# NSA attention on one Trainium2 core: two compressed softmaxes of the second query half moved later, and output banks begun by their first product

## Chip, cores and metric

The kernel runs on one core of one Trainium2 chip. The metric is the device time of one execution in microseconds (us); lower is better.

## What is computed

A trunk of four layers (256 tokens, width 1024, fp32) with a mixer, an MLP and a gate per layer. Only the second layer's mixer, NSA attention, is touched by the change. Cut to what matters:

```python
def nsa_attention(h, w_in, cmp_pe, cmp_w1, cmp_w2, w_out, rel_bias):
    proj = h @ w_in                       # q: 16 heads of 64; k, v for three branches, 4 groups; gates
    kc = compress(k_cmp, ...); vc = compress(v_cmp, ...)      # 15 compressed blocks
    s_c = einsum(qc, kc) * scale + b_c
    p_c = masked_softmax(s_c, m_c)
    o_c = einsum(p_c, vc)
    ...                                   # selected blocks: 4 blocks, all taken
    p_s = masked_softmax(s_s, m_s); o_s = einsum(p_s, v_g)
    p_w = masked_softmax(s_w, m_w); o_w = einsum(p_w, vw)     # window of 512, holds all 256 tokens
    return gate0 * o_c + gate1 * o_s + gate2 * o_w            # then @ w_out
```

## The kernel before, in words

The four query heads of two groups form a query half `ap` (0 or 1), the 256 tokens two tiles `t` of 128 queries. An **item** (`ap`, `t`, `j`) is one pair of heads in one tile: its first part takes the scores of the selected and the window branch for both heads (L1002, two matmuls into two `acc` banks) and their softmaxes (`soft`: on DVE an addition of the bias that also gives the row maximum, L497, two per bank; on ACT the exponential, L501). Its second part comes three items later: DVE makes the gated reciprocals (L1008, L1010) and multiplies (L1019), PE transposes (L1022, into `wk` banks), ACT copies (L1024), PE multiplies by the values (L1031) into the output bank `po4[ap, t]` (a `pj` bank), which takes all four items of a half and tile. Items of tile 0 have 128 keys (score rows of 256 columns for the two branches), those of tile 1 have 256 (512 columns). In order of issue: 0 (0,0,0), 1 (0,0,1), 2 (0,1,0), 3 (0,0,2), 4 (0,1,1), 5 (0,0,3), 6 (0,1,2), 7 (0,1,3), 8 (1,1,0), 9 (1,1,1), 10 (1,0,0), 11 (1,1,2) and so on.

The **compressed softmax** of a half and tile (`cmp_soft`, called s`ap``t` below) has PE take eight small score products (L956), DVE add the bias (L959, twice), take the minimum (L963), subtract (L964), ACT exponentiate (L965), DVE sum (L967), invert (L968), gate (L969) and multiply (L973, twice); a second step, t`ap``t`, transposes on PE (L979) and copies on ACT (L980). `finish` adds the compressed branch's product (L1038) to the output bank and splits the bank into two parts (L755 on ACT, L756 on DVE).

Work that belongs to no item is issued between items by a table, `FILL`: after item number n it issues the pieces named there: s and t as above, q1 (half of the query projection of the second half: 48 matmuls, L173 to L175 into a `pj` bank, and ACT's copy L944), p (a part of the projection of the next gate, 6 matmuls L173 to L175 into an `acc` bank, copied by ACT at L1142), c, g, d (the compression), O (loads of the output weights, split by ACT L150 and DVE L151). Each engine runs its instructions in one order; a scheduler that knows priorities and estimated durations sets it from the order of issue, so a change of the table also moves other instructions. Banks (`acc` 4, `pj` 2, `wk` 2) are taken in turn: a matmul into a bank waits for the last reader of what was there before.

Before the change the first matmul of an output bank (L1013) is a product of zeros over all 512 columns, with `start=True`; all later ones add.

Of the kernel before, what the change touches and what calls it, by code (L numbers as in the profile page):

```python
# [23 lines left out]
HD = 64  # L24
# [9 lines left out]
PACC = {0: 1, 1: 1, 2: 1, 3: 1}  # L34
PCB = 2
CW = 2
FILL = {-2: 'q0.c.p.q0.c', 1: 'p.g', 2: 'd0.q1.s01.d1', 3: 's00', 4: 't00.q1', 5: 's10.p.s11', 6: 'p', 7: 't01', 11: 't11.t10.O', 16: 'p'}
NORM = {0: 1, 1: 2, 2: 3, 3: 3}
MEP = 1
BANKS = dict(acc=('acc', 4), pj=('pj', 2), wk=('wk', 2))  # L40
# [40 lines left out]
def backwards(v):  # L81

    *rest, (step, n) = [list(z) for z in v.ap]
    return bass.AP(tensor=v.tensor, offset=v.offset + step * (n - 1), ap=[*rest, [-step, n]])


class Trunk:
# [533 lines left out]
    def scores(self, q, k, qs, w):  # L621
# [5 lines left out]
                self.nc.tensor.matmul(sc[c][:, hh * w : (hh + 1) * w], q[cs, hh, qs], k[cs, hh, :w], start=True, stop=True)  # L627
        return sc

    def pipeline(self, items):  # L630

        live = []
        for it in items:
            live.append(it)
            live = [g for g in live if next(g, self) is not self]
        while live:
            live = [g for g in live if next(g, self) is not self]
# [203 lines left out]
    def nsa(self, i, hT):  # L841
        nc, a = self.nc, self.a
# [15 lines left out]
        vs = [va[:, 0], va[:, 1]]  # L858
# [27 lines left out]
        def fill(n):  # L886
            for z in FILL.get(n, "").replace(".", " ").split():
                if z[0] == "c":
                    if "ph" not in cmp:
                        cmp["ph"] = self.cpsum()  # L890
                        cmp["up"] = self.compress_up(blks, cmp["ph"])
                    next(cmp["up"])
                elif z[0] == "g":
                    cmp["hid"] = self.compress_gelu(cmp["ph"])
                elif z[0] == "d":
                    self.compress_down(int(z[1]), cmp["hid"], (kcT, vcd)[int(z[1])])
                elif z[0] == "s":
                    soft2[z[1:]] = cmp_soft(int(z[1]), int(z[2]), qt[int(z[1])])
                    next(soft2[z[1:]])
                elif z[0] == "t":  # L900
                    next(soft2[z[1:]])
                    soft2[z[1:]] = None
                elif z[0] == "q":
                    next(qs[int(z[1])])
                elif z[0] == "p":
                    next(self.ple)
                elif z[0] == "Q":
                    q_load(int(z[1]))
                elif z[0] == "O":
                    self.early.append(self.unit(self.w_out, len(self.early), 1, 0, D))  # L910
            if n > 0:
                for ap, t in last:
                    if (ap, t) in po4 and soft2.get(f"{ap}{t}", 1) is None and n >= last[ap, t] + DP[i]:
                        finish(ap, t)

        qt, po4, soft2 = {}, {}, {}
        last = {(z[0], z[1]): n + 1 for n, z in enumerate(ORDN)}
        cmp = {}
        blks = [self.compress_blocks(kind, kvT[:, 2 * kind : 2 * kind + 2, :]) for kind in range(2)]
# [70 lines left out]
        def item(ap, t, j, qt, nbs):  # L990


            nk = t + 1
            w = nk * P
            qs = slice(t * P, (t + 1) * P)
            sc = self.acc()
            es = self.es([P, 2, 2, w])
            m, s = self.small([P, 4]), self.small([P, 4])
            rows = (j, j ^ 1)
            for g2, r in enumerate(rows):  # L1000
                hs = slice(g2 * HD, (g2 + 1) * HD)
                nc.tensor.matmul(sc[g2][:, : 2 * w].rearrange("p (z k) -> p z k", z=2), qt[hs, r, qs], ksw[hs, ap, :, :w], start=True, stop=True)  # L1002
            for g2, r in enumerate(rows):
                zs = slice(2 * g2, 2 * g2 + 2)
                self.soft(es[:, g2], lambda b: sc[g2][:, b * w : (b + 1) * w], 2, lambda b: backwards(nbs[g2][:, r, :w]), m[:, zs], s[:, zs])
            for _ in range(DP[i]): yield
            rs = self.small([P, 2, 2])
            nc.vector.reciprocal(rs.rearrange("p a b -> p (a b)"), s)  # L1008
            h0, h1 = 8 * ap + rows[0], 8 * ap + 4 + rows[1]
            nc.vector.tensor_tensor(rs, rs, gate[:, t, h0 : h1 + 1 : h1 - h0, 1:3], op=ALU.mult)  # L1010
            if (ap, t) not in po4:
                po4[ap, t] = self.pj()
                nc.tensor.matmul(po4[ap, t], self.zero[0:1, :], self.zero[0:1, 0:1].to_broadcast([1, 512]), start=True, stop=False)  # L1013
            ats = []
            for g2 in range(2):
                e = es[:, g2]
                pt = self.wk()
                for z in range(2):
                    nc.vector.tensor_scalar(e[:, z, :], e[:, z, :], rs[:, g2, z : z + 1], None, op0=ALU.mult)  # L1019
                    for kb in range(nk):  # L1020
                        zz = (z * nk + kb) * P
                        nc.tensor.transpose(pt[:, zz : zz + P], e[:, z, kb * P : (kb + 1) * P], self.ident)  # L1022
                at = self.m2([P, 2, nk, P])
                nc.scalar.activation(at.rearrange("p a b c -> p (a b c)"), pt[:, : 2 * w], AF.Copy)  # L1024
                ats.append(at)
            for z in range(2):
                for kb in range(nk):
                    for g2, r in enumerate(rows):
                        g = 2 * ap + g2
                        ov = po4[ap, t][(r % 2) * HD : (r % 2 + 1) * HD, (2 * g2 + r // 2) * P : (2 * g2 + r // 2 + 1) * P]  # L1030
                        nc.tensor.matmul(ov, vs[kb][:, z, g * HD : (g + 1) * HD], ats[g2][:, z, kb, :], start=False, stop=False)  # L1031

        def finish(ap, t):
            rows = slice(ap * HD, (ap + 1) * HD)
            for g2 in range(2):
                for r in range(4):
                    ov = po4[ap, t][(r % 2) * HD : (r % 2 + 1) * HD, (2 * g2 + r // 2) * P : (2 * g2 + r // 2 + 1) * P]
                    nc.tensor.matmul(ov, vcd[rows, 2 * ap + g2, :], pcT[rows, t, r, :], start=False, stop=g2 == 1 and r > 1)  # L1038
            self.split_out(po4.pop((ap, t)).rearrange("p (a b) -> p a b", a=4), oT, 4 * ap, 4, t)
# [7 lines left out]
        def items():  # L1047
            n = 0
            nbs = {}
            fill(-1)  # L1050
            for ap, t, j in ORDN:
                if ap not in nbs:
                    nbs[ap] = [self.bias_load(8 * ap + 4 * g2) for g2 in range(2)]
                yield item(ap, t, j, qt[ap], nbs[ap])
                n += 1
                fill(n)
            yield fin()
# [198 lines left out]
```

## Time and profile before

| | us |
|---|---|
| three runs, median (lowest to highest) | 1389.82 (1389.5 to 1394.78) |
| the profiled execution, its own time | 1391.37 |
| its span in the trace | 1389.5 |
| PE busy in it | 1370.0 |
| DVE busy | 906.8 |
| ACT busy | 757.3 |
| the NSA attention stage in the trace | about 397 to 490 |

A span is the time from the first to the last instruction of the trace. Busy is the time in which an engine had an instruction under way. The trace counts two records for one fp32 matmul whose product is taken with 64 rows or 64 columns of the array (an item's score products, its value products), so that a pair of score products shows as x4.

### The profile page before, as it was taken

The page shows a single profiled execution, that of the slowest core. Times are in us where ns is not written, and L with a number is a line of the kernel's source. Part 1 is how long each engine was busy: PE and PEld are TensorE (multiplying, and loading weights), DVE is VectorE, ACT ScalarE, POOL GpSimd, SP SyncE. Part 2 cuts the span into 40 slices and gives each one's busy share as a digit, 9 for nine tenths or more (in the row PEclk, how much of TensorE's full clock was granted, in tenths as well). Part 3 has the DMA queues.
Part 4 walks back from the last instruction along what each step waited for, and adds up shares of the span by engine and source line. Part 5 has one row for each costly group of instructions (what it writes and reads, how often), then busy time and mean ns, then how long its engine had stood idle before and what let it go on. Part 6 is the DMA issues. An engine that isn't in the chain of part 4 may idle for free.

```text
span 1389.5 us, 20335 instructions
## 1 busy us (share of the span) xinstructions
PE 1370.0 (99%) x7604; PEld 1137.7 (82%) x7604; DVE 906.8 (65%) x1636; ACT 757.3 (55%) x1268; POOL 53.3 (4%) x101
## 2 busy tenths in 40 slices
PE   8999999999999999999999999999999999999998
PEld 6987888888976688888878878888888987888887
DVE  6677765667557666666575566766576677766655
ACT  6555555455446845454465665545556566554443
POOL 1011000002000000000010000000001011000000
PEclk9999999999999999999999999999999999999999
DMA  8844765546673046565466625656554753665642
GB/s 280 264 139 156 235 200 184 182 155 188 186 263 111 21 139 222 168 210 176 129 212 202 220 75 184 215 184 198 191 182 128 232 165 103 219 210 172 203 140 76
DMA packets 144526, 247.28 MB, mean 178 GB/s; under 512 B 10195, under 2 KB 101243, under 8 KB 144428
## 3 DMA queue, kind: packets, MB, share of 16 engines
q1 hardware_dynamic: 134848, 235.26, 52.5%
q10 hardware_dynamic: 9580, 10.73, 2.5%
q8 instruction: 60, 0.98, 0.3%
q14 instruction: 38, 0.31, 0.1%
HBM read 243.81 MB, written 1.10 MB: 176 GB/s over the span
## 4 chain that ended last, share of the span: by engine, by line
PE 88%; issue 5%; DVE 2%; ACT 2%; POOL 2%; DMA 1%; DVEq 0%; POOLq 0%; ACTq 0%
PE pj L182 13%; PE acc L173 13%; PE acc L174 13%; PE acc L175 13%; PE pj L183 7%; PE pj L173 6%; PE pj L175 6%; PE pj L174 6%; PE wk L256 2%; PE pj L1031 1%; PE acc L627 1%; DVE wl L151 1%; PE wk L1022 1%; PE acc L1002 1%; PE wk L744 1%
## 5 line engine op out<-in xcount | busy, mean ns | idle before, releaser
L151 DVE TENSOR_TENSOR wl<-raw,wh 128x1024 fp32r<-128x1024 f32 x421 | 510.5, 1221 | 227.7 <-ACT wh L150 215.1
L150 ACT ACTIVATE wh<-raw 128x1024 fp32r<-128x1024 f32 x421 | 443.7, 1059 | 224.3 <-PE acc L174 106.3
L182 PE MATMUL pj<-big,wh 128*128 128x512 f32 x768 | 274.1, 401 | 0.0
L183 PE MATMUL pj<-big,wl 128*128 128x256 f32 x768 | 215.4, 281 | 0.0
L173 PE MATMUL acc<-wh,s 128*128 128x512 f32 x512 | 200.3, 392 | 0.0
L175 PE MATMUL acc<-wl,s 128*128 128x512 f32 x512 | 199.5, 390 | 0.0
L174 PE MATMUL acc<-wh,s 128*128 128x512 f32 x512 | 199.3, 390 | 0.0
L182 PEld LDWEIGHTS pj<-big,wh 128*128 128x128 f32 x768 | 144.2, 188 | 38.1 <-DVE m L1076 3.6
L183 PEld LDWEIGHTS pj<-big,wl 128*128 128x128 f32 x768 | 145.0, 189 | 0.9
L173 PE MATMUL pj<-big,wh 128*128 128x256 f32 x480 | 138.3, 288 | 0.5 <-ACT wh L150 0.5
L174 PE MATMUL pj<-big,wl 128*128 128x256 f32 x480 | 136.9, 285 | 0.5 <-DVE wl L151 0.5
L175 PE MATMUL pj<-big,wh 128*128 128x256 f32 x480 | 137.0, 285 | 0.0
L173 PE MATMUL acc<-wh,big 128*128 128x512 f32 (+2 forms) x344 | 131.2, 381 | 2.2 <-ACT wh L150 2.2
L174 PE MATMUL acc<-wh,big 128*128 128x512 f32 (+2 forms) x344 | 130.4, 379 | 0.0
L175 PE MATMUL acc<-wl,big 128*128 128x512 f32 (+2 forms) x344 | 129.9, 380 | 0.3
L175 PEld LDWEIGHTS acc<-wl,s 128*128 128x128 f32 x512 | 96.1, 188 | 20.5
L173 PEld LDWEIGHTS acc<-wh,s 128*128 128x128 f32 x512 | 96.1, 188 | 20.3 <-ACT s L1080 0.3
L174 PEld LDWEIGHTS acc<-wh,s 128*128 128x128 f32 x512 | 96.2, 188 | 19.4 <-DVE s L1081 0.2
L173 PEld LDWEIGHTS pj<-big,wh 128*128 128x128 f32 x480 | 92.4, 193 | 3.1 <-issue 1.2
L174 PEld LDWEIGHTS pj<-big,wl 128*128 128x128 f32 x480 | 92.3, 192 | 2.0 <-DVE wl L151 1.1
L175 PEld LDWEIGHTS pj<-big,wh 128*128 128x128 f32 x480 | 92.4, 192 | 0.3
L501 ACT ACTIVATE s<-s,small 128x128 f32<-128x128 f32 (+1 forms) x160 | 70.9, 447 | 33.8 <-DVE small L497 23.4
(238 smaller groups left out, 1748.4 us busy)
## 6 DMA issues: line engine op xcount, KB each, us to landing
raw<-in_mlp_w_dram SPq DMA_DIRECT2D x256, 512.0 KB, 4.7
raw<-in_da_w_in_dram SPq DMA_DIRECT2D x48, 512.0 KB, 5.1
raw<-in_ple_gate_w_dram SPq DMA_DIRECT2D x32, 512.0 KB, 4.2
raw<-in_fox_w_in_dram SPq DMA_DIRECT2D x24, 512.0 KB, 4.4
raw<-in_nsa_w_in_dram SPq DMA_DIRECT2D x18, 512.0 KB, 4.0
raw<-in_da_w_out_dram SPq DMA_DIRECT2D x16, 512.0 KB, 3.9
g<-in_norm_g_dram SPq DMA_DIRECT2D x15, 512.0 KB, 5.8
nb<-row ACTq DMA_DIRECT2D x12, 512.0 KB, 6.6
```

The costliest lines, as they stand in the source:

```text
L150: self.nc.scalar.activation(wh, w, AF.Copy),
L151: self.nc.vector.tensor_tensor(wl, w, wh.bitcast(F32), op=ALU.subtract),
L173: mm(out, l[0], r[0], start=first, stop=False)
L174: mm(out, l[1], r[0], start=False, stop=False)
L175: self.mms.append(mm(out, l[0], r[1], start=False, stop=last))
L182: mm(out.rearrange("p (z n) -> p z n", z=2), l[0], aT[2][:, :, k, :], start=first, stop=False)
L183: mm(out[:, :S], l[1], a, start=False, stop=last)
L256: z = nc.tensor.transpose(pt[:, c * P : (c + 1) * P], src[:, (b + c) * P : (b + c + 1) * P], self.ident)
L501: nc.scalar.activation(e[:, b, :], e[:, b, :], AF.Exp, bias=m[:, b : b + 1], scale=-1.0, accum_out=s[:, b : b + 1])
L627: self.nc.tensor.matmul(sc[c][:, hh * w : (hh + 1) * w], q[cs, hh, qs], k[cs, hh, :w], start=True, stop=True)
L744: nc.tensor.matmul(po[c * HD : (c + 1) * HD, hh * P : (hh + 1) * P], vs[kb][:, h * HD : (h + 1) * HD], at[:, hh, kb, :], start=kb == 0, st ...
L1002: nc.tensor.matmul(sc[g2][:, : 2 * w].rearrange("p (z k) -> p z k", z=2), qt[hs, r, qs], ksw[hs, ap, :, :w], start=True, stop=True)
```

## The change

The pieces s10 and s11, which stood behind item 5 with a gate part between them, now stand behind items 7 and 9, each alone. The product of zeros is left out; the first value product into each half of the output bank's partitions (`r % 2` picks the half) has `start=True`, and `behind` tells the scheduler, for each other product of that half, to keep it behind that first one on PE.

```diff
-FILL = {-2: 'q0.c.p.q0.c', 1: 'p.g', 2: 'd0.q1.s01.d1', 3: 's00', 4: 't00.q1', 5: 's10.p.s11', 6: 'p', 7: 't01', 11: 't11.t10.O', 16: 'p'}
+FILL = {-2: 'q0.c.p.q0.c', 1: 'p.g', 2: 'd0.q1.s01.d1', 3: 's00', 4: 't00.q1', 5: 'p', 6: 'p', 7: 't01.s10', 9: 's11', 11: 't11.t10.O', 16: 'p'}
...
+    def behind(self, a, b):
+
+        self.tc.add_manual_dep(b.ins, a.ins.name, mybir.DependencyInfo(mybir.DependencyClass.NoSync, mybir.DependencyReason.DATA), reason="clears the bank")
...
             if (ap, t) not in po4:
-                po4[ap, t] = self.pj()
-                nc.tensor.matmul(po4[ap, t], self.zero[0:1, :], self.zero[0:1, 0:1].to_broadcast([1, 512]), start=True, stop=False)
+                po4[ap, t], head[ap, t] = self.pj(), {}
...
-                        nc.tensor.matmul(ov, vs[kb][:, z, g * HD : (g + 1) * HD], ats[g2][:, z, kb, :], start=False, stop=False)
+                        first = r % 2 not in head[ap, t]
+                        m = nc.tensor.matmul(ov, vs[kb][:, z, g * HD : (g + 1) * HD], ats[g2][:, z, kb, :], start=first, stop=False)
+                        if first:
+                            head[ap, t][r % 2] = m
+                        else:
+                            self.behind(head[ap, t][r % 2], m)
```

Lines of the changed kernel are 3 to 9 higher: L956 is L960 there, L959 L963, L963 L967, L964 L968, L965 L969, L967 L971, L968 L972, L969 L973, L973 L977, L979 L983, L1002 L1006, L1008 L1012, L1010 L1014, L1019 L1022, L1022 L1025, L1031 L1035, L1038 L1047, L755 L759, L756 L760.

The order of PE around item 4's scores (`acc_883`, `acc_884`); `pj_877` is the bank of the 48 matmuls of q1's second half, `acc_888` and `acc_893` are banks of a gate part, `wk_867` takes item 0's transposes, `pj_866` is the output bank of half 0, tile 0, `wk_876` takes t00. Before:

```order
L828 MATMUL wk_854_4059<-mid_853_4057,m2_825_3932 128x64 x2
L956 MATMUL wk_861_4083<-s4_708_3283,s4_791_3718 128x64 x4
L173 MATMUL pj_877_4146<-big_661_3061,wh_835_3964 128x256
L174 MATMUL pj_877_4146<-big_661_3061,wl_836_3965 128x256
L175 MATMUL pj_877_4146<-big_661_3061,wh_835_3964 128x256
```

After the change, the same place:

```order
L832 MATMUL wk_854_4059<-mid_853_4057,m2_825_3932 128x64 x2
L960 MATMUL wk_861_4083<-s4_708_3283,s4_791_3718 128x64 x4
L1006 MATMUL acc_883_4216<-s4_764_3569,s4_791_3718 128x512
L1006 MATMUL acc_884_4217<-s4_764_3569,s4_791_3718 128x512
L173 MATMUL acc_888_4231<-wh_816_3903,m2_799_3796 128x512
L174 MATMUL acc_888_4231<-wh_816_3903,m2_800_3797 128x512
L1025 MATMUL wk_867_4106<-ident_3_65,s4_812_3888 128x128
```

The 48 matmuls into `pj_877` stood ahead of item 4's scores; they now stand behind them, behind five of the six matmuls of the gate part and behind item 0's transposes and products.

DVE around s10 (`mid_913`, with its scores in `wk_914`) in the changed kernel; `acc_923` is the first bank of item 7, `small_918` the gated reciprocal of item 4, which are normalised in `s4_885`:

```order
L963 TENSOR_TENSOR mid_913_4335<-wk_914_4336,s4_708_3283 128x60 x2
L967 TENSOR_REDUCE small_915_4343<-mid_913_4335 128x8
L968 TENSOR_TENSOR mid_913_4335<-mid_913_4335,small_915_4343 128x120
L971 TENSOR_REDUCE small_916_4347<-mid_913_4335 128x8
L1012 RECIPROCAL small_918_4355<-small_887_4220 128x4
L497 ISA s4_925_4386,small_926_4387<-acc_923_4384,nb_808_3882 128x256
L497 ISA small_926_4387 128x1
L972 RECIPROCAL small_916_4347<-small_916_4347 128x8
L1014 TENSOR_TENSOR small_918_4355<-small_918_4355,s4_708_3283 128x4
L497 ISA s4_925_4386,small_926_4387<-acc_923_4384,nb_808_3882 128x256
```

Before the change, s10 (`mid_888`) and s11 (`mid_894`) stood side by side on DVE, behind item 4's softmaxes, with no item's softmax between them; now s10's chain stands ahead of both softs of item 7's first bank.

PE around s11 (scores in `wk_941`) in the changed kernel; `acc_961` is item 10's second bank, `acc_976` item 11's first, which takes the bank of item 9's first, `pj_866` is being finished by L1047:

```order
L1035 MATMUL pj_866_4105<-m2_934_4418,s4_712_3294 64x128
L960 MATMUL wk_941_4440<-s4_708_3283,s4_846_3986 128x64
L1047 MATMUL pj_866_4105<-s4_763_3568,s4_708_3283 64x128 x8
L1006 MATMUL acc_961_4543<-s4_764_3569,s4_846_3986 128x256
L1006 MATMUL acc_976_4615<-s4_764_3569,s4_846_3986 128x512
L1025 MATMUL wk_946_4472<-ident_3_65,s4_909_4316 128x128 x4
```

s11's scores stood with s10's, six items earlier; they now stand in the middle of item 5's products. On DVE the chain of s11 stands ahead of item 9's first softs, between the softs of item 8's two banks and the split of the finished output bank (L760).

## Rows read from the trace of the kernel before

**Rows 1.** The page, part 1: busy time, share of the span, instructions.

```profile
PE 1370.0 (99%) x7604; PEld 1137.7 (82%) x7604; DVE 906.8 (65%) x1636; ACT 757.3 (55%) x1268; POOL 53.3 (4%) x101
```

**Rows 2.** Windows of the stage: from:to, length, busy of PE, PEld, DVE, ACT, POOL, granted clock, DMA.

```profile
426.00:440.00 14.00, 12.22 (x73) 7.83 (x74) 9.95 (x49) 7.66 (x27) 0.66 (x2) 0.91 0.38 123
440.00:455.00 15.00, 14.89 (x103) 8.23 (x99) 10.54 (x56) 11.35 (x40) 0.31 (x1) 0.97 0.22 71
455.00:470.00 15.00, 15.00 (x128) 9.72 (x127) 10.95 (x60) 13.51 (x45) 0.00 (x0) 1.00 0.01 2
```

**Rows 3.** PE's timeline: start, length of the group, then the idle time before it.

```profile
415.00 1.06 PE L956 MATMUL wk<-s,s 128*128 128x64 f32 x8
...
421.79 1.13 PE L1002 MATMUL acc<-s,s 64*128 64x512 f32 x4
423.34 0.30 PE L1022 MATMUL wk<-ident,s 128*128 128x128 f32 x1 [0.42 <-DVE s L1019]
...
429.06 0.43 PE L1031 MATMUL pj<-m,s 128*64 128x128 f32 x2 [0.31 <-ACT m L1024]
...
433.52 1.88 PE L1002 MATMUL acc<-s,s 64*128 64x512 f32 x4
436.80 1.36 PE L1022 MATMUL wk<-ident,s 128*128 128x128 f32 x8 [1.40 <-DVE s L1019]
438.18 2.70 PE L1031 MATMUL pj<-m,s 128*64 128x128 f32 x16
...
447.06 1.42 PE L1002 MATMUL acc<-s,s 64*128 64x512 f32 x4
...
459.47 1.09 PE L1031 MATMUL pj<-m,s 128*64 128x128 f32 x16
```

**Rows 4.** Windows of one us with PE idle, and after them.

```profile
346.00:347.00 1.00, 0.31 (x2) 0.00 (x0) 0.63 (x1) 0.00 (x0) 0.84 (x4) 1.00 0.53 119
435.00:436.00 1.00, 0.40 (x1) 0.00 (x0) 0.90 (x8) 0.30 (x1) 0.00 (x0) 1.00 0.00 0
438.00:439.00 1.00, 0.94 (x5) 0.38 (x6) 0.80 (x7) 0.87 (x3) 0.00 (x0) 0.50 0.00 0
712.00:713.00 1.00, 0.00 (x0) 0.00 (x0) 0.00 (x0) 0.25 (x1) 0.63 (x2) 1.00 1.04 332
715.00:716.00 1.00, 1.00 (x5) 0.81 (x4) 0.94 (x1) 1.00 (x4) 0.00 (x0) 0.50 0.76 270
```

**Rows 5.** The chain of waits: start, length, what held the end there.

```profile
427.21 0.32 PE pj L1013
450.60 0.62 PE acc L1002 x2
451.81 1.02 PE pj L1038 x16
455.07 1.05 PE acc L1002 x2
```

**Rows 6.** DVE's timeline: the chain of s00 and s01, softs, a reciprocal, a bank's split.

```profile
411.28 0.35 DVE L959 TENSOR_TENSOR mid<-wk,s 128x60 f32<-128x60 f32 x2 [0.86 <-PE wk L956]
412.68 0.27 DVE L963 TENSOR_REDUCE small<-mid 128x8 f32<-128x120 f32 x1
413.95 0.20 DVE L968 RECIPROCAL small<-small 128x8 f32<-128x8 f32 x1
416.83 0.42 DVE L497 CUSTOM_DVE_ANT_0 s<-acc,nb 128x256 f32<-128x256 f32 x1
418.57 0.27 DVE L963 TENSOR_REDUCE small<-mid 128x8 f32<-128x120 f32 x1
...
444.03 0.17 DVE L1008 RECIPROCAL small<-small 128x4 f32<-128x4 f32 x1
444.51 0.42 DVE L497 CUSTOM_DVE_ANT_0 s<-acc,nb 128x256 f32<-128x256 f32 x1
454.54 0.69 DVE L756 TENSOR_TENSOR big<-pj,big 128x512 fp32r<-128x512 f32 x1 [0.54 <-ACT big L755]
```

More of the change, by code (lines that the diff above doesn't have):

```diff
@@ L914, in fill @@
                         finish(ap, t)
-        qt, po4, soft2 = {}, {}, {}
+        qt, po4, head, soft2 = {}, {}, {}, {}
         last = {(z[0], z[1]): n + 1 for n, z in enumerate(ORDN)}
```

## The prediction

> **What bounds the kernel now.** I read the busy times first: PE is busy for 1370.0 of 1389.5 us, DVE for 906.8, ACT for 757.3 [rows 1]. The end is PE's, so a change counts for what it takes off PE, or for the time that PE stands still. The change touches one stage, so I read that one by windows [rows 2]: from 426 to 440 PE is busy for 12.22 of 14 us at a granted clock of 0.91, from 440 to 455 for 14.89 of 15, from 455 to 470 for all 15. PE thus has something over 2 us to win before 440 and next to nothing after it; whatever makes it wait after 440 is a loss. PE's timeline [rows 3] tells which waits make up the first part: 0.42 us for item 0's normalisation, 0.31 for ACT's copy of item 1, 0.75 inside item 6's score pair (1.88 long where a pair takes 1.13: the second product waited for its bank), and 1.40 for item 2's normalisation, which on DVE stood behind the two compressed softmaxes. After the last one the clock fell: the window at 438 has a granted clock of 0.50, which is the 1.2 GHz level [rows 4], and the 16 records of L1031 took 2.70 us where the same group takes 1.09 later [rows 3], 1.61 us lost.
>
> **Zeros.** Four products of zeros go. The chain holds three of them, 0.32 us each [rows 5]; the fourth isn't on the chain and is taken as worth nothing. The product that takes over `start=True` was there before. So -0.32 in the front part and -0.64 behind it. If PE waits at those places anyway, they give nothing.
>
> **The front part (416 to 441).** By the order of the changed kernel, q1's 48 matmuls no longer stand between s01's scores and item 4's. In the trace they ran while DVE did the softs of items 2 and 3 and s00's chain. Without them:
> - item 4's second bank is free when the last soft of item 2 is done, 416.83 + 0.42 = 417.25 [rows 6], while PE is through with L956 at 415.00 + 1.06 = 416.06 [rows 3]: 1.2 us of waiting.
> - The pair ends 1.05 later, at 418.3 [rows 5], as a 512-column product alone does. Then comes a gate part, whose bank is free after two softs of item 3. These stand on DVE behind s00's L967. Its L963 starts at 418.57; from L963 to L968 the chain takes 413.95 - 412.68 = 1.27 (with ACT's exponential in it), so they begin at 419.85 and are done by 420.7 at 0.42 each [rows 6]: 2.4 us of waiting.
> - the waits for normalisation and copy of 0.42 and 0.31 stay, about 0.7.
> - item 5's two score products come apart (0.62 more, since two side by side take about what one takes alone: 1.13 and 1.05), and so do item 6's (1.05 more) [rows 3, 5].
>
> That is 1.2 + 2.4 + 0.7 + 0.62 + 1.05 = 6.0. Gone are 0.42 + 0.31 + 0.75 + 1.40 + 1.61 and a zero's 0.32, 4.8 in all. Net **+1.2**, with -1.0 if the small waits hide behind each other and the split pairs. q1's work itself and the weight splits queued on DVE and ACT only change place; the split weights are needed after the stage's end.
>
> **s10.** Its scores on PE stand behind t01, and its chain on DVE stands ahead of both softs of item 7's first bank. Item 9's first score product needs that bank. From the scores on: two L959 0.35, L963 to L968 1.27, then the pattern reciprocal, soft, reciprocal, soft, which is seen once already: 444.51 + 0.42 - 444.03 = 0.90 [rows 6]. With under 0.1 between them, 2.6 us. PE's only work meanwhile is item 8's pair, 1.06. So PE waits 1.5, and item 9's products come apart, 2.10 against 1.42 [rows 3, 5]: **+2.2**. Queued behind on DVE are item 4's normalisations, whose transposes come after item 9's product on PE, so they add little. If DVE's small steps overlap better than those of s00, the wait is 1.0; if item 7's softs are late by PE's own delay, it is 2.
>
> **s11.** The same once more, with more in the chain: two L959 0.35, two softs of item 8 at up to 0.42 each, L963 to L968 1.27, one ACT exponential of item 8 ahead of s11's (some 0.5), the pattern of 0.90, and the split of a finished bank, 0.69 [rows 6], that stands between the two softs. In all 4.5 us. PE's cover is L1038, 1.02, and one score product, 0.62 [rows 5]. So PE waits 2.9, and the pair of items 10 and 11 comes apart, +0.6: **+3.5**. The lower bound, with ACT's queue empty and the bank's split overlapped, is 1.7 for the wait.
>
> After 460 PE is full in both orders [rows 2], so nothing is won back there. Sum without the clock: -0.64 + 1.2 + 2.2 + 3.5 = +6.3, of which the front is the least sure.
>
> **The clock.** What a wait of 1.4 us did in this stage, a fall to 0.50, is the row that is nearest to what the new waits would do. Another wait, with PE idle for all of the window at 712, was also followed by 0.50, at 715; a stretch with 0.69 us idle, at 346, I take as the other end, since no half clock followed there [rows 4]. New waits of 1.5, 2.4 and 2.9 us lie in reach of the first two. A fall costs 1.6. I take one as sure enough to count, after the longest: +6.3 + 1.6 = +7.9, less 0.2 for the part of it that lies in other waits. Against the median 1389.82 that is **1397.5**. (The profiled execution took 1391.37, 1.55 over the median; the difference is put on the median.) The Trainium skill, page "TensorE: Matmul & The Clock Gate", section "HAM oscillation — how this bites in real kernels", speaks of longer gaps than these as what throttles TensorE; by that rule none of the waits would lower the clock and the sum would be the one without it. The trace doesn't bear this out: 1.40 us were enough ahead of the window at 438 [rows 3, 4].
>
> **Rivals.**
> - *The clock falls after all three waits*: +6.3 + 3 x 1.6 = 11.1, so 1400.9. For it: both idle stretches of this length that I quote were followed by half clock. Against it: half-clocked PE work before a wait makes the wait shorter.
> - *No fall*: 1396.1. For it, the skill's rule above, and that the front's wait comes in two pieces with work between. Against it, [rows 4].
> - *The chains are hidden* (the other side). If DVE has s10's and s11's chains done within PE's cover, that is in 1.06 and 1.64 us, and item 3's softs come ahead of s00's chain, nothing new appears; then the front's 0.42 + 0.31 + 0.75 + 1.40 + 1.61 and three zeros are won, 5.4 us: 1384.4. It decides by whether the chain from L959 to the second soft is under 1.1 us. For it: the split of the two chains frees item 2's normalisation, which is the longest wait of the stage. Against it: the exponential alone makes L963 to L968 1.27.
> - *Only the zeros count*: the new waits lie where PE would have waited in other ways (q1 later covers what it covered earlier), 1389.82 - 0.96 = 1388.9.
>
> **Chances.** One or two falls, 1397.5 to 1399.1: 0.42. Three: 0.13. None: 0.17. Chains hidden: 0.10. Only zeros, or the front's gain cancelling part of the waits, 1389 to 1393: 0.18. What a measurement here can tell from no change is about 0.5%, 6.9 us: from 1382.9 to 1396.8 counts as the same. Slower takes three quarters of the first case, nearly all of the second and a third of the third, 0.50; faster takes 0.06, a little over half of the hidden chains; the same has 0.44. The range leaves out most of the hidden chains and the top of the three falls: 1388.5 to 1401.5.
>
> **What would show it.** In the profile after: no rows of L1013; PE idle before the first L1006 of item 9 for about 1.5 us and before item 11's first for about 2.9, both ended by DVE's L497; PE idle before the gate part's L173 near 418 to 421; hardly any wait before item 2's transposes; single L1006 products where there were pairs; windows at 0.50 behind the waits. The prediction is wrong if PE goes from 440 to 470 as full as before, or if the wait before item 2's transposes is still there.

## The result: slower by 1.1%, about twice as far as forecast

The changed kernel takes 1404.78 us (median of six runs, 1403.98 to 1408.48); the kernel before, 1389.59 beside it. The ratio is 1.0112, 95% interval 1.0093 to 1.0130. In time that is 15 us, where 7.7 was forecast and 1401.5 was the top of the range. The direction was right, the size was not.

The profiled execution of the changed kernel is the longest of its six, 1408.48; some 2 us of it were lost ahead of the change's place (the first L956, now L960, starts at 412.01 and not at 410.18). Its page, part 1, the line of the engines; it answers to [rows 1]:

```profile
PE 1381.2 (98%) x7600; PEld 1143.1 (81%) x7600; DVE 907.1 (64%) x1636; ACT 757.1 (54%) x1268; POOL 52.8 (4%) x101
```

PE has four instructions less and is busy for 11 us more: its instructions got longer. The windows of the stage tell why; they answer to [rows 2] (columns as there, the granted clock is the third number from the end):

```profile
410.00:426.00 16.00, 13.39 (x78) 10.79 (x77) 13.05 (x56) 7.34 (x23) 0.00 (x0) 0.82 0.60 229
426.00:440.00 14.00, 13.60 (x85) 10.05 (x84) 6.62 (x18) 8.64 (x20) 0.31 (x1) 0.93 0.28 81
440.00:455.00 15.00, 13.46 (x71) 7.07 (x70) 10.34 (x56) 9.36 (x32) 0.46 (x2) 0.90 0.38 120
455.00:470.00 15.00, 12.74 (x69) 7.88 (x68) 5.83 (x33) 5.64 (x18) 0.00 (x0) 0.73 0.08 26
470.00:490.00 20.00, 20.00 (x143) 13.05 (x142) 11.57 (x59) 14.89 (x50) 0.00 (x0) 0.85 0.00 1
```

PE stands still in three places, where the forecast put them, and the clock falls in or behind each. PE's timeline, which answers to [rows 3]:

```profile
418.61 1.81 PE L1006 MATMUL acc<-s,s 64*128 64x512 f32 x4 [0.56 <-DVE small L497]
422.46 0.79 PE L173 MATMUL acc<-wh,m 128*128 128x512 f32 x1 [2.04 <-DVE small L497]
...
435.89 0.93 PE L1035 MATMUL pj<-m,s 128*64 128x128 f32 x8 [0.40 <-ACT m L1027]
...
440.01 1.09 PE L1025 MATMUL wk<-ident,s 128*128 128x128 f32 x8
...
450.46 1.12 PE L1006 MATMUL acc<-s,s 64*128 64x512 f32 x2 [1.54 <-DVE small L497]
...
465.60 2.07 PE L1006 MATMUL acc<-s,s 64*128 64x512 f32 x2 [2.16 <-DVE small L497]
467.60 1.97 PE L1025 MATMUL wk<-ident,s 128*128 128x128 f32 x8
...
480.00 1.09 PE L1025 MATMUL wk<-ident,s 128*128 128x128 f32 x8
```

The reader is to see two things. The waits are 0.56, 2.04, 1.54 and 2.16 us, 6.3 together, and item 2's transposes, at 440.01, wait for nothing any more. And a group of eight transposes takes 1.97 us at 467.60 where a like group takes 1.09 at 480.00. Windows of one us give the clock, as in [rows 4]:

```profile
421.00:422.00 1.00, 0.00 (x0) 0.00 (x0) 0.63 (x6) 0.30 (x1) 0.00 (x0) 0.60 0.24 33
424.00:425.00 1.00, 1.00 (x5) 0.70 (x4) 0.93 (x6) 0.43 (x2) 0.00 (x0) 0.50 0.00 0
457.00:458.00 1.00, 1.00 (x10) 0.86 (x8) 0.00 (x0) 0.00 (x0) 0.00 (x0) 0.50 0.03 9
466.00:467.00 1.00, 1.00 (x2) 0.10 (x1) 1.00 (x5) 0.18 (x2) 0.00 (x0) 0.50 0.00 0
474.00:475.00 1.00, 1.00 (x6) 0.98 (x6) 0.00 (x0) 0.00 (x0) 0.00 (x0) 0.50 0.00 0
```

Half clock (1.2 GHz) reigns from 421.2, within the wait of 2.04 us, to 428.0, from 451.9 to 458.8 and from 465.6 to 475.8. One minus the granted clock, summed over the one-us windows, is 3.4, 3.4 and 5.1 us, 11.9 in all, against 1.7 for the fall behind item 2's wait before. (Both profiles have one more fall of 1.7 us, ahead of the places that the change touches; the last section comes back to it.)

The mean granted clock of whole runs says the same without any profile. The median over the changed kernel's runs is 0.989, over the 22 runs of the kernel before (beside the first experiments) 0.997. Times a span of some 1400 us that is 15.4 against 4.2 us of lost clock. Of the 15 us that the change costs, about 11 are clock and about 4 are the waits and split pairs themselves. (A step of 0.001 in the clock is 1.4 us, so the split is good to a microsecond or so.)

### The profile page after: what moved, and what is told of

Read it like the earlier page. It is cut to its first block, busy times and chain, and to the rows that moved or that the text cites. A ratio compares the mean times of both kernels' runs of the same rounds, so it can differ in the third digit from the quotient of the medians.

```text
span 1406.7 us, 20329 instructions
## 1 busy us (share of the span) xinstructions
PE 1381.2 (98%) x7600; PEld 1143.1 (81%) x7600; DVE 907.1 (64%) x1636; ACT 757.1 (54%) x1268; POOL 52.8 (4%) x101
## 4 chain that ended last, share of the span: by engine, by line
PE 86%; issue 5%; DVE 3%; ACT 2%; DMA 2%; POOL 2%; SPq 0%; ACTq 0%; DVEq 0%; POOLq 0%
PE pj L182 13%; PE acc L173 13%; PE acc L174 13%; PE acc L175 13%; PE pj L183 6%; PE pj L173 6%; PE pj L174 6%; PE pj L175 6%; PE wk L256 2%; PE pj L1035 1%; DMA raw<-in_da_w_in_dram 1%; PE acc L1006 1%; PE acc L627 1%; PE wk L1025 1%; DVE wl L151 1%
```

## Experiments

Theory A: the banks and the table each bring waits of their own, and most of the loss is the half clock behind the waits. Its rivals: the late softmaxes carry everything (B), the banks do (C), the half clock costs nothing, since PE would wait anyway (D). Ratios are against the kernel before, run beside each.

For reading the edits: a number in the table counts the items issued so far. With the items numbered from 0, a piece under number n is therefore issued just ahead of item n, and where the text has s10 "behind item 5" it stands between items 4 and 5. s11 moves from number 5 to number 9, by four items.

**Only the table** (from the kernel before; zeros stay):

```diff
-5: 's10.p.s11', 6: 'p', 7: 't01', 11:
+5: 'p', 6: 'p', 7: 't01.s10', 9: 's11', 11:
```

> Only the table is changed: s10 behind item 7, s11 behind item 9, products of zeros as before. By its order q1's 48 matmuls stay ahead of item 4's scores. Theory A (each edit brings its own waits, and the clock falls after each of them): the waits of 1.5 and 2.2 us and half clock after both, 3.4 and 5.0 us lost there as in the changed kernel, less the 1.40 us wait and the 1.7 us of half clock that item 2's normalisation cost before: +8 to +11 us. Theory B (the moved softmaxes carry everything): +15. Theory C (the output banks carry most, by the order they give PE): under +4.

Measured: 1396.91 us, ratio 1.0052 (1.0038 to 1.0065), +7.8 us by the medians. Its PE row at s11's wait, then two windows:

```profile
454.29 0.58 PE L1013 MATMUL pj<-zero 1*128 1x512 bf16 x1 [1.67 <-DVE big L756]
```

```profile
455.00:470.00 15.00, 15.00 (x59) 8.69 (x60) 8.12 (x42) 6.74 (x24) 0.00 (x0) 0.50 0.00 1
470.00:490.00 20.00, 20.00 (x167) 13.43 (x166) 13.12 (x70) 16.18 (x50) 0.00 (x0) 0.99 0.01 2
```

One wait of 1.67 us, here for the split of a finished bank that the next product of zeros had to take, and the clock was at half until 470: 8.5 us lost by the windows. The wait at s10 was 0.69 only, since in this order its scores stand ahead of item 7's second product, and no fall followed. So the table alone costs half of the loss. A's mechanism holds, a little under the +8 to +11 it gave and with one fall of 8.5 us in place of its two of 3.4 and 5.0; B and C don't hold.

**Only the banks** (the changed kernel with the old table):

```diff
-5: 'p', 6: 'p', 7: 't01.s10', 9: 's11', 11:
+5: 's10.p.s11', 6: 'p', 7: 't01', 11:
```

> Only the output banks are changed: no products of zeros, first product with start; s10 and s11 behind item 5 as before. By its order q1's 48 matmuls stand behind item 4's scores, as in the changed kernel. Theory A: PE waits some 0.6 and 2.0 us ahead of item 4's second bank and of the gate part, half clock after them (3.4 us lost), item 2's wait of 1.4 us stays in some size; less 1 us of zeros: +4 to +6 us. Theory B: -1 (the zeros alone), no new wait. Theory C: +10 or more.

Measured: 1392.67 us, ratio 1.0022 (1.0007 to 1.0037), +3.5 us. PE's timeline has the two waits of the front, and item 2's, 1.07, besides:

```profile
416.00 1.81 PE L1006 MATMUL acc<-s,s 64*128 64x512 f32 x4 [0.57 <-DVE small L497]
419.86 0.50 PE L173 MATMUL acc<-wh,m 128*128 128x512 f32 x1 [2.04 <-DVE small L497]
```

To take products of zeros away should not cost anything; this edit does, since the scheduler then puts q1's 48 matmuls behind item 4's scores (the runs that move q1 show it below). Whether the missing zeros or the order kept by `behind` makes the scheduler do so was not tried. The waits of A are there; the loss is a little under its +4 to +6. In this profile the half clock lasted from 421.3 to 424.7 only, 1.7 us lost; but the profiled run is the fastest of its eleven (1390.12, granted clock 0.998, the others down to 0.994), so the median run lost more. The two edits alone cost 7.8 and 3.5 us, together 15; by the profiles three falls stand in the combination where each alone had one.

**One softmax at a time** (from the kernel before):

```diff
-5: 's10.p.s11', 6: 'p', 7: 't01', 11:
+5: 'p.s11', 6: 'p', 7: 't01.s10', 11:
```

> Only s10 is moved, behind item 7; s11 stays behind item 5, zeros stay. Theory A: a wait of some 1.5 us ahead of item 9's first scores, and half clock after it; item 2's wait shrinks, since one compressed chain is gone ahead of it: +2 to +5 us. Theory B: about half of +15.

```diff
-5: 's10.p.s11', 6: 'p', 7: 't01', 11:
+5: 's10.p', 6: 'p', 7: 't01', 9: 's11', 11:
```

> Only s11 is moved, behind item 9; s10 stays behind item 5, zeros stay. Theory A: a wait of some 2.2 us ahead of item 11's first scores and half clock after it for 5 us lost; item 2's wait shrinks: +4 to +8 us. Theory B: about half of +15.

Measured: s10 alone 1391.32, ratio 1.0017 (1.0008 to 1.0026), +2.2 us; s11 alone 1394.97, ratio 1.0032 (1.0016 to 1.0049), +5.8 us. Waits of 1.54 and 1.66 us; item 2's wait shrank to 0.18 and 0.17. Both times lie within A. B's 7.5 is far from the first and outside the interval of the second (2.2 to 6.8 us). The two together make 8.0, about what the table alone costs (7.8).

**The waits filled.** This is the run that tells the clock from the waits. To the changed kernel it adds 42 transposes whose results nobody reads.

```diff
+KEEP = {(0, 0, 0): 14, (0, 1, 1): 12, (0, 1, 2): 16}
...
                 pt = self.wk()
+                for z in range(KEEP.get((ap, t, j), 0) if g2 == 0 else 0):
+                    nc.tensor.transpose(pt[:, :P], self.ident, self.ident)
```

> The changed kernel, with 42 transposes of the identity that nobody reads added on PE: 14 ahead of item 0's transposes, 12 ahead of item 4's, 16 ahead of item 6's, each into the bank that the real transposes overwrite. They stand at the three waits (0.6 and 2.0, 1.5, 2.2 us) and fill most of them; about 1 us of the front's second wait stays, as the scheduler puts its 14 ahead of item 4's scores. Theory A (the waits themselves cost some 4 us, the half clock behind them some 10 us more): the half-clock stretches go, and although PE has 5.3 us more to do the time falls to +3 to +7 us over before, from +15. Theory D (the waits cost it, the half clock only shows that DVE is late and PE would wait then anyway): no gain, +15 or more.

Measured: 1394.55 us, ratio 1.0042 (1.0029 to 1.0054). With 5.2 us more to do (the three groups of transposes take 1.72, 1.53 and 1.97), PE ends 10 us sooner than in the changed kernel. Its windows, then its timeline at the waits:

```profile
410.00:426.00 16.00, 14.34 (x108) 12.13 (x108) 11.97 (x53) 7.12 (x23) 0.31 (x1) 0.98 0.50 191
426.00:440.00 14.00, 13.62 (x90) 9.54 (x88) 9.44 (x32) 10.46 (x27) 0.00 (x0) 1.00 0.48 152
440.00:455.00 15.00, 15.00 (x90) 8.79 (x90) 7.52 (x41) 8.27 (x28) 0.46 (x2) 1.00 0.24 79
455.00:470.00 15.00, 14.25 (x123) 9.71 (x119) 11.74 (x62) 10.74 (x37) 0.00 (x0) 1.00 0.00 1
```

```profile
416.84 1.72 PE L1023 MATMUL wk<-ident 128*128 128x128 f32 x14 [0.21 <-DVE s L844]
...
421.07 0.50 PE L174 MATMUL acc<-wh,m 128*128 128x512 f32 x1 [1.45 <-DVE small L498]
...
445.00 1.53 PE L1023 MATMUL wk<-ident 128*128 128x128 f32 x12
...
456.67 1.97 PE L1023 MATMUL wk<-ident 128*128 128x128 f32 x16
...
459.69 1.12 PE L1007 MATMUL acc<-s,s 64*128 64x512 f32 x2 [0.43 <-DVE small L498]
```

No window of the stage after the fills is under full clock (the 0.98 in the first is the end of an earlier fall). Median granted clock 0.998. The transposes do not save waiting: with the waits for DVE that are left (0.21, 1.45, 0.43) they fill 7.3 us where the changed kernel waited 6.3. Yet the time fell by 10, close to the 11.9 of half clock that went less this 1.0. What is left of the loss, 5.7 us, is the fills, the remaining waits and the split pairs. D falls: the half clock is a cost of its own, and the larger one.

**q1 ahead of item 4 again**, everything else as changed:

```diff
-3: 's00', 4: 't00.q1', 5: 'p',
+3: 's00.q1', 4: 't00', 5: 'p',
```

> The changed kernel, with q1's piece moved from behind item 4 to behind item 3, so that its 48 matmuls stand ahead of item 4's scores again; s10 and s11 late, banks begun by their first product. Theory A: the front's waits and the half clock after them go (3 to 6 us), the two waits at s10 and s11 stay with theirs: +6 to +10 over before. Theory B (the late softmaxes carry all): stays at +15.

Measured: 1393.70 us, ratio 1.0033 (1.0020 to 1.0045), +4.8 us, 1.2 below the interval of A's forecast. The front's waits are gone, s10's is 0.69, s11's 2.16. The row behind the latter has half clock already:

```profile
453.88 2.07 PE L1006 MATMUL acc<-s,s 64*128 64x512 f32 x2 [2.16 <-DVE small L497]
```

So where q1 stands decides over about 11 of the 15 us (1404.78 against 1393.70), and over s10's wait too, 0.69 against 1.54, because item 7's second product moves with it.

**The banks, with q1 in its place**, and the compressed softmaxes where they were:

```diff
-5: 'p', 6: 'p', 7: 't01.s10', 9: 's11', 11:
-3: 's00', 4: 't00.q1',
+5: 's10.p.s11', 6: 'p', 7: 't01', 11:
+3: 's00.q1', 4: 't00',
```

> Banks begun by their first product, s10 and s11 behind item 5 as in the kernel before, q1's piece behind item 3. If the banks' loss came only from q1's matmuls standing behind item 4's scores, none of the new waits is there and the zeros are won: 0 to -3 us against before. If the first product with start costs something by itself: slower than before by over 1 us.

Measured: 1385.98 us, ratio 0.9979 (0.9968 to 0.9990), 2.9 us faster than the kernel before. The first product with `start` costs nothing by itself. Three zeros account for 1.0 of the 2.9, and the wait of 0.42 ahead of item 0's transposes is gone; the rest was not traced. Item 2's wait of 1.40 us and its fall, from 436.2 to 439.6, are still there. Against the run before this one, 1393.70, it also gives the price of the two late softmaxes with q1 ahead of item 4: 7.7 us, as the table alone cost (7.8). So the two edits simply add up there, and what they cost together beyond their sum, 4 us, comes with q1's place.

**As that, with s11 one item after s10:**

```diff
-5: 's10.p.s11', 6: 'p',
+5: 's10.p', 6: 's11.p',
```

> As the one before, with s11 one item later than s10 (behind items 5 and 6), so that the two chains no longer stand together on DVE ahead of item 2's normalisation. Theory A: item 2's wait of 1.4 us shrinks below what makes the clock fall, no new wait above 1 us: -1 to -5 us against before. If any compressed chain ahead of an item's softs makes a wait that lowers the clock: +2 or more.

Measured: 1386.74 us, ratio 0.9991 (0.9975 to 1.0008): no difference that can be told. Item 2's wait shrank to 0.18, but item 3's transposes then waited 1.66 us, and half clock of 3.4 us followed:

```profile
439.35 1.05 PE L1025 MATMUL wk<-ident,s 128*128 128x128 f32 x4 [1.66 <-DVE s L1022]
```

The wait moved to where s11's chain now stands; ten of eleven runs lie between 1384.89 and 1387.57, one at 1398.41 with a granted clock of 0.988. The first half of A's forecast held, the second didn't.

**Real work in the wait:**

```diff
-5: 's10.p.s11', 6: 'p',
+5: 's10.s11', 6: 'p.p',
```

> Banks begun by their first product, q1's piece behind item 3, s10 and s11 both behind item 5 and both gate parts (12 matmuls) behind item 6, so that real work of PE stands where it waited for item 2's normalisation. Theory A: that wait of 1.40 us goes, and the half clock after it too (1.7 us): 4 to 6 us faster than before, and runs closer together, since no run has a fall there. Theory D (the clock is no cost of its own): 1 us less than the variant without it, so 3 to 4 faster.

Measured: 1385.19 us, ratio 0.9966 (0.9953 to 0.9979), 4.3 us faster than the kernel before and 20 faster than the changed one. This is the lowest median of the study. Its windows from 410, then the row of item 2's transposes, whose wait was 1.40:

```profile
410.00:426.00 16.00, 15.36 (x113) 12.72 (x112) 14.23 (x57) 11.07 (x28) 0.46 (x2) 1.00 0.63 231
426.00:440.00 14.00, 13.37 (x76) 8.30 (x76) 9.56 (x50) 8.20 (x28) 0.00 (x0) 1.00 0.32 109
440.00:455.00 15.00, 14.89 (x114) 8.91 (x114) 12.10 (x68) 12.96 (x46) 0.31 (x1) 1.00 0.22 71
455.00:470.00 15.00, 15.00 (x123) 9.74 (x121) 10.89 (x57) 13.09 (x44) 0.00 (x0) 1.00 0.01 2
```

```profile
434.36 1.15 PE L1025 MATMUL wk<-ident,s 128*128 128x128 f32 x8 [0.18 <-DVE s L1022]
```

Twelve matmuls that were needed anyway, six more than in the version with the banks and q1 alone, stand where PE waited; the clock of the stage is at 1.00 throughout in this profile, and the runs lie within 1384.55 and 1386.38. As evidence for the clock it is weak: 4.3 lies within A's 4 to 6 and just over D's 3 to 4, its interval (2.9 to 6.5 us) holds both, and it overlaps with that of the version with the banks and q1 alone (1.4 to 4.4). That the wait and its fall are gone is shown; that this made the version faster than that one is not.

**Dense work behind a wait**, to see what ends the half clock; from the version with q1 earlier and s10, s11 late:

```diff
+KEEP = {(0, 1, 3): 24}
```

> The variant with q1's piece behind item 3 and s10, s11 late (its half clock after s11's wait lasted 9.6 us), with 24 transposes of the identity that nobody reads added on PE ahead of item 7's transposes, some 4 us behind that wait. They are 3.0 us of work at full clock, 6 at half. Theory E (the half clock lasts as long as PE's work behind the wait is score and value products on half of the array, and dense work ends it): the half clock ends within the transposes or right behind them, and the time is at most 3 us over that variant. Theory F (the length has nothing to do with what PE runs): half clock of 9 us and more as before, the transposes cost 3 to 6 us in full.

Measured: 1392.47 us, ratio 1.0022 (1.0011 to 1.0033). With 3 us more of PE work it is not slower than without (1393.70, ratio 1.0033). In its profile the half clock ended at 460, after 6.8 us, where it was 10.2 without. That speaks against F, though from one profile each: over all runs the granted clock is much the same, median 0.9955 against 0.995. And when the half clock ended only 3 of the 24 transposes had run, so it doesn't show E either.

## Why the prediction missed

- **The waits** were forecast by place, cause and nearly by size: 1.2 and 2.4 us in the front against 0.56 and 2.04, 1.5 against 1.54 at s10, 2.9 against 2.16 at s11. The wait of item 2, the zeros and the pairs went as said; of the 0.7 of small waits that were to stay, 0.40 did. Here is s10's chain on DVE in the changed kernel, as it was added up from [rows 6]:

```profile
447.89 0.34 DVE L963 TENSOR_TENSOR mid<-wk,s 128x60 f32<-128x60 f32 x2 [1.57 <-PE wk L960]
448.27 0.28 DVE L967 TENSOR_REDUCE small<-mid 128x8 f32<-128x120 f32 x1
448.58 0.28 DVE L968 TENSOR_TENSOR mid<-mid,small 128x120 f32<-128x120 f32 x1
449.24 0.28 DVE L971 TENSOR_REDUCE small<-mid 128x8 f32<-128x120 f32 x1 [0.37 <-ACT mid L969]
449.43 0.17 DVE L1012 RECIPROCAL small<-small 128x4 f32<-128x4 f32 x1
449.52 0.39 DVE L497 CUSTOM_DVE_ANT_0 s<-acc,nb 128x256 f32<-128x256 f32 x1
...
449.98 0.42 DVE L497 CUSTOM_DVE_ANT_0 s<-acc,nb 128x256 f32<-128x256 f32 x1
```

  From 447.89 to 450.40 is 2.5 us; 2.6 was forecast. s11's chain ran from 461.66 to 465.54, 3.9 where 4.5 was forecast: its exponential waited hardly any longer on ACT than s10's, and the softs follow each other at 0.35 and not 0.42.
- **Waits, pairs and zeros together** came out too high. The +6.3 had the fall of before already taken off; without that it was +7.9. By the granted clock of the runs they cost about 4; by the version with filled waits about 4.7, its 5.7 less the 1.0 by which the fills and what is left of the waits exceed the waits that were there. Of the difference the front's waits are 1.0, s11's 0.7 and the small waits 0.3; the rest was not traced further. Alone this step would have put the forecast too high, and so it hid a part of the next one.
- **The clock is the step that failed**: "A fall costs 1.6. I take one as sure enough to count". With the fall of before taken off, the forecast had a net clock term of nothing, and 11 us were measured. Both factors were too small, the price more than the count. The clock fell at all three waits, which stood as a rival with 0.13; three falls at 1.6 make 4.8. But a fall cost 3.4, 3.4 and 5.1 us and not 1.6, 11.9 in all. The price was read from a single fall, [rows 3], as if it were a constant of the chip. It is not: by the windows of the runs a fall at these waits cost from 1.7 to 8.5 us. With three falls at 11.9 less the 1.7 that were there before, and 4 us of waits, the sum would have been 14.
- "Half-clocked PE work before a wait makes the wait shorter", held against three falls, was no brake: the stretches ended before the next wait began (428.0 and 448.9; 458.8 and 463.4).
- The Trainium skill's page "TensorE: Matmul & The Clock Gate", section "HAM oscillation — how this bites in real kernels", would have let all of these waits pass. The runs say otherwise: waits of 1.40 to 2.16 us were followed by 1.2 GHz in ten of the eleven kernels that had one.

## What to carry to other kernels

Where PE sets the end, a wait of one to two us on it can have two prices, the wait and the half clock behind it, and the second can be several times the first; in these runs the second price went when work filled the wait, even work that nobody needed. One fall in a trace does not give its price. A compressed chain on another engine costs little where PE has dense work to do meanwhile, and much where the next product waits for a bank that is read behind that chain. When an edit changes what a scheduler may place, compare the order on every engine: an edit that took four small products away (and kept an order among others) moved 48 matmuls that it did not name and cost 3.5 us, and moving one piece in the table gave that and more back.

## What was not expected of the hardware

How long the half clock lasts after a wait differed widely, in work of much the same kind. Read from one-us windows of one profile each:

| kernel | the wait, us | half clock behind it, us |
|---|---|---|
| before | 1.40 | 3.4 |
| changed: front, s10, s11 | 2.04, 1.54, 2.16 | 6.8, 6.8, 10.2 |
| only the table, s11 | 1.67 | 17.1 |
| only the banks, front; item 2 | 2.04; 1.07 | 3.4; none |
| only s10; only s11 | 1.54; 1.66 | 6.8; 13.7 |
| waits filled, front | 1.45 | none |
| q1 earlier, s11 | 2.16 | 10.2 |
| banks and q1, item 2 | 1.40 | 3.4 |
| spread by one, item 3 | 1.66 | 3.4 |
| dense work behind s11's wait | 2.16 | 6.8 |

The length doesn't go with the length of the wait. PE was busy all through these stretches by the records, mostly with score and value products, which use half of the array's rows or columns, and with transposes. Those in the front ended within 0.2 us of the start of q1's 48 matmuls (424.7 against 424.5; 428.0 against 428.2, where the matmuls came after, so that they did not end it); those of 10 us and more all lie behind s11's wait, where there is nothing but item work. Whether it is the kind of work that holds the clock down, or the moment at which it fell, stays open; the run with dense work behind the wait had a shorter stretch and is no proof.

Nor does it take a wait of over a us. In eight of the twelve profiles, the kernel before among them, the clock is at half for 3.4 us between 405 and 412 (1.7 us lost), ahead of every place that the edits touch, and the longest wait of PE in the 20 us ahead of it is 0.50. In the other four, where the longest wait is as long (0.49 to 0.50), it stays full. The kernel before, then only the banks:

```profile
408.00:409.00 1.00, 1.00 (x7) 1.00 (x6) 0.41 (x3) 0.68 (x1) 0.00 (x0) 0.50 1.00 410
408.00:409.00 1.00, 0.95 (x8) 0.74 (x7) 0.99 (x3) 0.79 (x1) 0.00 (x0) 1.00 1.01 385
```

So the length of one wait does not settle whether the clock falls, and profiles of two kernels can differ by 1.7 us of clock where no edit reached. The losses of the changed kernel are clear of that; differences of 1 to 2 us between the better versions are not.
